# Order edges for an expert selection and full-row masks for attention and SSD scores in a two-block transformer kernel

## The chip, the cores and the metric

One core of a Trainium2 chip runs the whole program. It has TensorE (PE, matmuls), VectorE (DVE), ScalarE (ACT), GpSimd (POOL) and SyncE (SP, which issues the transfers here). The metric is the time of one execution on the device in microseconds; beside it the profiler has a span, from the first to the last instruction of one profiled execution. TensorE's granted clock is given as a share of 2.4 GHz; 0.5 is 1.2 GHz.

## The reference

One sequence of T = 256 tokens of width D = 1024 in float32 goes through two blocks, with modulation by a vector `c` in both.

```
def reference(x, ...):
    # block 1
    h  = modulate(rms_norm(x), sh1, sc1);  z = h @ w_in + b_in
    ym = mlstm(conv(mq, mk), mv, mi, mf) * sigmoid(mo)          # 4 heads of 128
    ya = moba_attention(rope(aq), rope(ak), av)                 # 8 heads of 64, one block of 256: causal softmax
    x += g1 * ((sigmoid(ga) * (ym @ p_mlstm) + sigmoid(gb) * (ya @ p_moba)) @ w_out)
    x += g2 * ((silu(h2 @ w_gate) * (h2 @ w_up)) @ w_down);  x = rms_norm(x)
    # block 2
    y_pool = pool_mixer(...)                                    # trailing-window means, 4 groups of 128
    y_ssd  = ssd_mixer(...)                                     # 16 heads of 64, two chunks of 128
        seg = a_cs[l] - a_cs[s];  decay = exp(where(l >= s, seg, -inf))
        y = (c @ b.T * decay) @ x + c @ states * exp(a_cs);  y = rmsnorm(y * silu(z))
    x += gate_m * (concat(y_pool, y_ssd) @ w_out_2)
    # PEER: 8 heads, two key tables of 128, 16384 experts
    q = h @ w_query
    v1, i1 = top_k(q1 @ keys1, 16);  v2, i2 = top_k(q2 @ keys2, 16)
    top_s, pos = top_k(v1[:, None] + v2[None, :], 16);  gates = softmax(top_s)
    x += gate_f * sum(gates * gelu(h . expert_down[idx]) * expert_up[idx]);  return rmsnorm(x)
```

## The kernel before

Nearly all of the time is matrix products with weights that are read once. SP's queue brings each weight tile, 128 x 1024 float32, to `raw` (or `ada`). Each is split: ScalarE copies it to `hi` in fp32r (L213), a rounded form of float32, and VectorE writes `lo`, the rest of `raw` less `hi` (L218). Where `cur["gp"]` is n, every n-th `lo` is made by GpSimd instead (L216). Then `proj` runs eight times three matmuls of 256 columns, `hi` by the activation's high part (L274), `hi` by its low part (L275) and `lo` by the high part (L276): 24 for a tile. The split of a tile is written two tiles ahead of its use (`LA` = 2), and the pools of `hi` and `lo` have three buffers each, so that `hi` of a tile can begin when TensorE is done with the third tile before it. `cur["lo"]` is the last `lo` of VectorE that has been written so far in the program.

In the program, smaller work is put between the weight tiles by generators: `tick()` advances the first generator in `gens` by one step, and it is called once for each tile. The order of the instructions on each engine is made by a scheduler out of a simulated timeline, and a helper `after(a, b)` adds an edge to it: `a` comes later than `b`; between instructions of one engine that is an order and no wait.

The change touches three such parts.

MoBA, `moba` (L659 on): for the second half of the tokens (`tt` = 1, 256 keys) and then the first (`tt` = 0, 128 keys), and for four pairs of heads `c`, a score of each head goes to one half `j` of a PSUM buffer `ps`. A head has 64 dimensions, and `ro` holds two heads above each other, so a score reads 64 of the 128 rows: the upper half for even `c`, the lower for odd (L671). A causal mask is added by a bfloat16 matmul of the identity with a triangle (L672). Maximum, exponential, transposes (L699 to L701), `PT` (L702) and the product with `va` (L709, L710) follow. `sg` are the gates, a sigmoid over 4096 columns on ScalarE (L107 is the helper of all exponentials and the like), and `ymH` the mLSTM's output for the product with `p_mlstm` (L731).

SSD (L860 on): for each of 16 heads a matmul over 48 rows of `ArS` selects and spreads the cumulated decays in 384 columns (L929), two bfloat16 matmuls add masks (L930, L931), and ScalarE makes the exponentials `M`. At the end of the stage come four pool products (L989), the outputs `mixS` (L1016), the sum of squares `accp` (L1021) that TensorE adds up over partitions (L1023, L1024), from it `lnt` and `srt`, with them `pv` (L1030) and `mixP` (L1031), which the last tiles of the stage multiply by weights.

PEER's selection: `topk(hq, tt)` is a generator for four heads and 128 tokens: eight rounds of max, index, replace, max, index over 128 scores (L1097 to L1101), `cand` with 256 sums for each head (L1108), four such rounds over `cand` (L1115 to L1119), index arithmetic, and the gates. There are four passes. They run beside the tiles of the query and of `dblock` (`expert_down`), 72 ticks in all; GpSimd takes part in the splits for a while. The gather stage, with `A` and `B` as one-hot masks, follows.

Of the kernel before, what the change touches and what calls it, by code (L numbers as in the profile page):

```python
# [9 lines left out]
F32 = mybir.dt.float32  # L10
# [51 lines left out]
def two_block_kernel(ctx, tc, I, out, dbg=None):  # L62
# [230 lines left out]
    gens = []  # L293

# [91 lines left out]
    with p1:  # L386
# [267 lines left out]
        identb = q1.tile([P, P], BF, name="identb")  # L654
        V.tensor_copy(identb, ident)
        trib = q1.tile([P, P], BF, name="trib")
        V.tensor_copy(trib, cs_("tri"))

        def moba():  # L659
# [4 lines left out]
            for tt in (1, 0):  # L664
                ns = (tt + 1) * P
                for c in range(4):
                    ps = sp()
                    rows = slice(64 * (c % 2), 64 * (c % 2) + 64)
                    for j in range(2):
                        r = 2 * (c // 2) + j  # L670
                        PE.matmul(ps[:, j * T:j * T + ns], ro[rows, r, tt * P:(tt + 1) * P], ro[rows, 4 + r, :ns], start=True, stop=False)  # L671
                        PE.matmul(ps[:, j * T + tt * P:j * T + ns], identb, trib, start=False, stop=True)  # L672
# [160 lines left out]
    with ExitStack() as p3:  # L833
# [48 lines left out]
        ArS = q3.tile([48, 384], F32R, name="ArS")  # L882
        id16 = q3.tile([48, 16], F32R, name="id16")
        S.activation(id16[0:32], ident[0:32, 0:16], AF.Copy)
        S.activation(id16[32:48], ident[0:16, 0:16], AF.Copy)
        identb = q3.tile([P, P], BF, name="identb")
        V.tensor_copy(identb, ident)
        trib = q3.tile([P, P], BF, name="trib")
        V.tensor_copy(trib, cs_("mB"))
# [32 lines left out]
        for i in (8, 9, 10, 11):  # L922
# [3 lines left out]
            for h in range(4 * i - 32, 4 * i - 28):  # L926
                ab = sp()
                se = id16[:, h:h + 1].to_broadcast([48, P])
                PE.matmul(ab[:, :384], se, ArS, start=True, stop=False, skip_group_check=True)  # L929
                PE.matmul(ab[:, :P], identb, trib, start=False, stop=False, skip_group_check=True)  # L930
                PE.matmul(ab[:, T:384], identb, trib, start=False, stop=True, skip_group_check=True)  # L931
# [142 lines left out]
    with ExitStack() as p4:  # L1074
# [8 lines left out]
        def topk(hq, tt):  # L1083
# [3 lines left out]
            for hf in range(2):  # L1087
# [8 lines left out]
                for h in range(4):  # L1096
                    V.max(v[:, h, 0:8], s_[:, h])  # L1097
                    V.max_index(x[:, h, 0:8], v[:, h, 0:8], s_[:, h])
                    V.match_replace(s_[:, h], v[:, h, 0:8], s_[:, h], -3.0e38)
                    V.max(v[:, h, 8:16], s_[:, h])  # L1100
                    V.max_index(x[:, h, 8:16], v[:, h, 8:16], s_[:, h])  # L1101
                    yield
# [5 lines left out]
            V.tensor_tensor(cand, vv[0].unsqueeze(3).to_broadcast([P, 4, 16, 16]),  # L1108
# [52 lines left out]
        for i in range(16):  # L1161
# [11 lines left out]
            if i == 7:  # L1173
                cur["gp"] = 2
                gens += [topk(0, 0), topk(0, 1)]
            elif i > 7:
                tick()
# [297 lines left out]
```

## Time and profile before

| | |
|---|---|
| median of 3 runs | 1427.33 us (1427.19 to 1429.57) |
| profiled execution, its own time | 1433.29 us |
| its span | 1431.5 us |
| mean granted clock | 0.989 |
| TensorE busy | 1389.7 us, 97%, 11842 matmuls |
| VectorE busy | 1155.1 us, 81% |
| ScalarE busy | 708.8 us, 50% |
| GpSimd busy | 61.3 us, 4% |
| transfers | 285.92 MB, 200 GB/s over the span |

TensorE's busy share is high over the whole, so that a change counts where it stands still or runs at half the clock: the slices of the page say where that is, the windows how much, and the waits for whom. The times of the tables are of one profiled execution, which took longer than the runs that are timed without a profile.

### The profile page before, as it was taken

How to read it: one execution, taken by the hardware profiler on the slowest of the kernel's cores; microseconds unless marked ns; L12 is line 12 of the kernel's file. 1: busy time of each engine (PE TensorE's matmuls, PEld its weight loads, DVE VectorE, ACT ScalarE, POOL GpSimd, SP SyncE). 2: the span in 40 equal slices, each digit the busy share in tenths (PEclk: the TensorE clock that was granted, in tenths of full speed). 3: DMA queues.
4: the chain of work that ended last, by engine and by line, in shares of the span. 5: the costliest groups of instructions: out<-in, count | busy, mean ns of one | idle time of the engine just before them, and what ended most of it. 6: DMA issues, size and time to landing. Idle time of an engine off the chain costs nothing.

```text
span 1431.5 us, 28913 instructions
## 1 busy us (share of the span) xinstructions
PE 1389.7 (97%) x11842; PEld 1341.2 (94%) x11842; DVE 1155.1 (81%) x1995; ACT 708.8 (50%) x1052; POOL 61.3 (4%) x50
## 2 busy tenths in 40 slices
PE   8999989999999999998899999999999999999997
PEld 6888779899999788998899999999999999999997
DVE  7999558988888597789956978989689999675554
ACT  4555465554546846555554544444444443444443
POOL 0000000000000000123420000000000000000001
PEclk9999889999999999999999999999999999999999
DMA  9988416699995353554455555555655555676663
GB/s 319 341 289 314 148 47 192 229 350 343 330 317 207 104 155 125 163 161 149 162 188 181 177 166 174 163 165 172 180 164 161 177 161 172 200 215 213 208 205 103
DMA packets 78921, 285.92 MB, mean 200 GB/s; under 512 B 8786, under 2 KB 9186, under 8 KB 78660
## 3 DMA queue, kind: packets, MB, share of 16 engines
q1 hardware_dynamic: 78484, 282.60, 60.6%
q8 instruction: 93, 1.52, 0.4%
q0 software_dynamic: 304, 1.47, 0.3%
q14 instruction: 40, 0.33, 0.1%
HBM read 282.99 MB, written 1.05 MB: 198 GB/s over the span
## 4 chain that ended last, share of the span: by engine, by line
PE 85%; DVE 10%; ACT 2%; DMA 2%; issue 1%; SPq 0%; DVEq 0%; ACTq 0%
PE pp L274 17%; PE pp L276 17%; PE pp L275 17%; PE sp L1271 9%; PE sp L1274 8%; PE sp L1275 8%; DVE lo L218 3%; PE pp L1210 2%; ACT hi L213 1%; PE sp L671 1%; DMA raw<-in_wst 0%; DVE raw L230 0%; DMA ada<-in_wst 0%; DVE M L965 0%; PE sp L929 0%
## 5 line engine op out<-in xcount | busy, mean ns | idle before, releaser
L213 ACT ACTIVATE hi<-raw 128x1024 fp32r<-128x1024 f32 x382 | 404.6, 1060 | 562.7 <-PE pp L275 282.9
L218 DVE TENSOR_TENSOR lo<-raw,hi 128x1024 fp32r<-128x1024 f32 x364 | 450.3, 1238 | 141.3 <-ACT hi L213 140.5
L276 PE MATMUL pp<-nH,lo 128*128 128x256 f32 x1064 | 301.6, 285 | 16.1 <-DVE lo L218 16.1
L274 PE MATMUL pp<-nH,hi 128*128 128x256 f32 x1064 | 300.0, 283 | 1.5 <-ACT fs L107 0.9
L275 PE MATMUL pp<-nL,hi 128*128 128x256 f32 x1064 | 300.3, 283 | 0.0
L1271 PE MATMUL sp<-wHL,hi 128*128 128x256 f32 x992 | 279.5, 283 | 0.0
L1274 PE MATMUL sp<-wHL,hi 128*128 128x256 f32 x992 | 277.7, 281 | 0.0
L1275 PE MATMUL sp<-wHL,lo 128*128 128x256 f32 x992 | 273.8, 281 | 0.0
L274 PE MATMUL pp<-hH,hi 128*128 128x256 f32 (+1 forms) x824 | 237.0, 288 | 1.3 <-ACT sg L721 1.3
L276 PE MATMUL pp<-hH,lo 128*128 128x256 f32 (+1 forms) x824 | 234.6, 285 | 0.0
L275 PE MATMUL pp<-hL,hi 128*128 128x256 f32 (+1 forms) x824 | 233.6, 284 | 0.0
L276 PEld LDWEIGHTS pp<-nH,lo 128*128 128x128 f32 x1064 | 200.2, 189 | 19.4 <-DVE lo L218 19.3
L274 PEld LDWEIGHTS pp<-nH,hi 128*128 128x128 f32 x1064 | 200.7, 189 | 2.1 <-ACT fs L107 1.1
L275 PEld LDWEIGHTS pp<-nL,hi 128*128 128x128 f32 x1064 | 200.5, 189 | 0.1
L1271 PEld LDWEIGHTS sp<-wHL,hi 128*128 128x128 f32 x992 | 188.2, 190 | 0.0
L1274 PEld LDWEIGHTS sp<-wHL,hi 128*128 128x128 f32 x992 | 188.0, 189 | 0.0
L1275 PEld LDWEIGHTS sp<-wHL,lo 128*128 128x128 f32 x992 | 185.9, 190 | 0.0
L274 PEld LDWEIGHTS pp<-hH,hi 128*128 128x128 f32 x824 | 157.1, 191 | 2.7 <-ACT sg L721 1.5
L276 PEld LDWEIGHTS pp<-hH,lo 128*128 128x128 f32 x824 | 157.2, 191 | 1.1 <-issue 0.7
L275 PEld LDWEIGHTS pp<-hL,hi 128*128 128x128 f32 x824 | 157.3, 191 | 0.7 <-issue 0.5
L1214 DVE SCALAR_TENSOR_TENSOR W<-pp,W 128x512 f32<-128x512 f32 x64 | 86.1, 1346 | 22.3 <-PE pp L1210 22.3
L213 ACT ACTIVATE hi<-ada 128x1024 fp32r<-128x1024 f32 x52 | 55.1, 1059 | 67.3 <-PE pp L275 37.9
(442 smaller groups left out, 2146.9 us busy)
## 6 DMA issues: line engine op xcount, KB each, us to landing
raw<-in_edn SPq DMA_DIRECT2D x128, 512.0 KB, 3.6
raw<-in_eup SPq DMA_DIRECT2D x128, 512.0 KB, 4.2
raw<-in_ada SPq DMA_DIRECT2D x64, 512.0 KB, 5.0
raw<-in_win SPq DMA_DIRECT2D x34, 512.0 KB, 4.4
ada<-in_ada SPq DMA_DIRECT2D x32, 512.0 KB, 5.1
raw<-in_wgu SPq DMA_DIRECT2D x32, 512.0 KB, 4.5
ada<-in_win SPq DMA_DIRECT2D x18, 512.0 KB, 4.5
raw<-in_wdn SPq DMA_DIRECT2D x15, 512.0 KB, 5.8
```

Of the source, the lines that this page charges most:

```text
L213: S.activation(hi, raw, AF.Copy)
L218: cur["lo"] = V.tensor_tensor(lo, raw, hi.bitcast(F32), OP.subtract)
L274: m = PE.matmul(ps, lh, rh, start=start, stop=False)
L275: PE.matmul(ps, lh, rl, start=False, stop=False)
L276: PE.matmul(ps, ll, rh, start=False, stop=stop)
L671: PE.matmul(ps[:, j * T:j * T + ns], ro[rows, r, tt * P:(tt + 1) * P], ro[rows, 4 + r, :ns], start=True, stop=False)
L1210: PE.matmul(ps[:, t * 64:(t + 1) * 64], A[:, t].rearrange("p n d -> p (n d)"), B[:, j, t].rearrange("p n d -> p (n d)"), start=(j == 0), s ...
L1214: V.scalar_tensor_tensor(wv, ps.rearrange("p (t n) -> p t n", t=GT), 1.0 / GSC, wv, OP.mult, OP.mult)
L1271: m = PE.matmul(o, hi[:, b], wH, start=first, stop=False, skip_group_check=True)
L1274: PE.matmul(o, hi[:, b], wL, start=False, stop=False, skip_group_check=True)
L1275: return PE.matmul(o, lo[:, b], wH, start=False, stop=last, skip_group_check=True)
```

## The change

```diff
+    def paced(ins):
+        after(ins, cur["lo"])
+        return ins
...
-        identb = q1.tile([P, P], BF, name="identb")
-        V.tensor_copy(identb, ident)
-        trib = q1.tile([P, P], BF, name="trib")
-        V.tensor_copy(trib, cs_("tri"))
+        identr = q1.tile([P, P], F32R, name="identr")
+        S.activation(identr, ident, AF.Copy)
+        trir = q1.tile([P, P], F32R, name="trir")
+        S.activation(trir, cs_("tri"), AF.Copy)
...
                 for c in range(4):
-                    ps = sp()
-                    rows = slice(64 * (c % 2), 64 * (c % 2) + 64)
-                    for j in range(2):
-                        r = 2 * (c // 2) + j
-                        PE.matmul(ps[:, j * T:j * T + ns], ro[rows, r, tt * P:(tt + 1) * P], ro[rows, 4 + r, :ns], start=True, stop=False)
-                        PE.matmul(ps[:, j * T + tt * P:j * T + ns], identb, trib, start=False, stop=True)
+                    if c % 2 == 0:
+                        pair = [sp(), sp()]
+                        for j in range(2):
+                            r = 2 * (c // 2) + j
+                            for i, ps in enumerate(pair):
+                                rows = slice(64 * i, 64 * i + 64)
+                                PE.matmul(ps[:, j * T:j * T + ns], ro[rows, r, tt * P:(tt + 1) * P], ro[rows, 4 + r, :ns],
+                                          start=j == 0, stop=False, skip_group_check=True)
+                        for ps in pair:
+                            PE.matmul(ps.rearrange("p (g s) -> p g s", g=2)[:, :, tt * P:ns], identr,
+                                      trir[:, None, :].to_broadcast([P, 2, P]), start=False, stop=True, skip_group_check=True)
+                    ps = pair[c % 2]
...
-        ArS = q3.tile([48, 384], F32R, name="ArS")
-        id16 = q3.tile([48, 16], F32R, name="id16")
+        ArS = q3.tile([P, 384], F32R, name="ArS")
+        id16 = q3.tile([P, 16], F32R, name="id16")
+        G.memset(ArS.bitcast(F32), 0.0)
+        G.memset(id16.bitcast(F32), 0.0)
...
-                se = id16[:, h:h + 1].to_broadcast([48, P])
+                se = id16[:, h:h + 1].to_broadcast([P, P])
                 PE.matmul(ab[:, :384], se, ArS, start=True, stop=False, skip_group_check=True)
-                PE.matmul(ab[:, :P], identb, trib, start=False, stop=False, skip_group_check=True)
-                PE.matmul(ab[:, T:384], identb, trib, start=False, stop=True, skip_group_check=True)
+                PE.matmul(ab.rearrange("p (g s) -> p g s", g=2)[:, :, :P], identr, trir[:, None, :].to_broadcast([P, 2, P]),
+                          start=False, stop=True, skip_group_check=True)
...
-                    V.max(v[:, h, 0:8], s_[:, h])
+                    paced(V.max(v[:, h, 0:8], s_[:, h]))
...
-                cur["gp"] = 2
+                cur["gp"] = 4
                 gens += [topk(0, 0), topk(0, 1)]
...
-            cur["gp"] = 2 if n2 < 28 else 0
+            cur["gp"] = 4 if n2 < 56 else 0
             dblock(n2)
             tick()
```

`paced` goes around all five instructions of a round over the scores, the first of each round over `cand`, `cand` itself, the first of the index arithmetic and of the gates, the first copy to `i1d`, and `A` of the gather stage. In SSD `identr` and `trir` are made as in MoBA, with the SSD's mask. The first eight tiles of the 72 are query tiles; `n2` counts the other 64. All lines behind the first edit move by 4 to 12, so that the row-half score is L677 after, the mask L680, the SSD unit L941 and L942, and the sum of squares L1035.

TensorE, at MoBA's scores, before: `ro` are the rotated queries and keys, `sp_` a PSUM buffer.

```order
L617 MATMUL sp_1293<-sq5_1291,ones_90 128x512
L671 MATMUL sp_1367<-ro_840 128x256
L672 LDWEIGHTS identb_1323
L672 MATMUL sp_1367<-trib_1325,identb_1323 128x128
L671 MATMUL sp_1367<-ro_840 128x256
```

The same place after, with the first of the following pieces of 128 columns:

```order
L621 MATMUL sp_1293<-sq5_1291,ones_90 128x512
L677 MATMUL sp_1367<-ro_840 128x256
L677 MATMUL sp_1368<-ro_840 128x256
L677 MATMUL sp_1367<-ro_840 128x256
L677 MATMUL sp_1368<-ro_840 128x256
L680 MATMUL sp_1367<-trir_1325,identr_1323 128x2x128
L680 MATMUL sp_1368<-trir_1325,identr_1323 128x2x128
...
L274 MATMUL pp_1939<-hH_85,hi_1875 128x256
L275 MATMUL pp_1939<-hL_86,hi_1875 128x256
L677 MATMUL sp_1467<-ro_840 128x128 x2
L680 MATMUL sp_1467<-trir_1325,identr_1323 128x2x128
```

Before, each score has its mask behind it. After, four scores go to two buffers in turn and two masks follow; the pieces of 128 columns come two to a buffer with projection matmuls (L274 to L276) between the buffers.

ScalarE, behind the scores, before:

```order
L702 ACTIVATE PT_1617<-sp_1623 128x384
L731 ACTIVATE ymH_2051<-hm_837 128x256 x2
L107 ACTIVATE sg_1327<-sg_1327 128x4096
L94 ACT_TABLE_LOAD
L107 ACTIVATE nfe_2068<-nfe_2068 128x8
```

and after:

```order
L712 ACTIVATE PT_1609<-sp_1615 128x384
L107 ACTIVATE sg_1327<-sg_1327 128x4096
L94 ACT_TABLE_LOAD
L107 ACTIVATE nfe_2060<-nfe_2060 128x8
L741 ACTIVATE ymH_2043<-hm_837 128x256 x2
```

The first two `ymH` have moved behind the sigmoid over `sg`.

VectorE, in the selection, from one split to the next, before (`v0`, `v1` are the values found, `x` their indices, `s` the scores):

```order
L218 TENSOR_TENSOR lo_7464<-raw_7461,hi_7463 128x1024
L1098 MAX_INDEX x0_7910<-v0_7909,s0_7902 128x8 x3
L1117 MATCH_REPLACE cand_7568<-ts__7602,cand_7568 128x256
L1098 MAX_INDEX x1_8069<-v1_8068,s1_8061 128x8 x3
L1117 MATCH_REPLACE cand_7568<-ts__7602,cand_7568 128x256
L1098 MAX_INDEX x1_8069<-v1_8068,s1_8061 128x8
L1117 MATCH_REPLACE cand_7568<-ts__7602,cand_7568 128x256 x2
L1099 MATCH_REPLACE s0_7902<-v0_7909,s0_7902 128x128 x4
L1118 MAX ts__7602<-cand_7568 128x8
L1099 MATCH_REPLACE s1_8061<-v1_8068,s1_8061 128x128 x2
L218 TENSOR_TENSOR lo_7538<-raw_7535,hi_7537 128x1024
```

and after, at the first `cand`:

```order
L218 TENSOR_TENSOR lo_7516<-raw_7513,hi_7515 128x1024
L1120 TENSOR_TENSOR cand_7546<-v0_7235,v1_7394 128x1024
L218 TENSOR_TENSOR lo_7552<-raw_7549,hi_7551 128x1024
L1127 MAX ts__7580<-cand_7546 128x8
L1128 MAX_INDEX po_7581<-ts__7580,cand_7546 128x8
L1129 MATCH_REPLACE cand_7546<-ts__7580,cand_7546 128x256
L1130 MAX ts__7580<-cand_7546 128x8
L218 TENSOR_TENSOR lo_7591<-raw_7588,hi_7590 128x1024
```

Before, two passes mix and 18 instructions stand between two splits; after, one step of one pass stands between them.

## Rows read from the trace of the kernel before

**Rows 1.** Page, 40 slices of 35.8 us, tenths
```profile
PE   8999989999999999998899999999999999999997
PEclk9999889999999999999999999999999999999999
```

**Rows 2.** Windows: length; busy PE, PEld, DVE, ACT, POOL; clock; DMA share; GB/s
```profile
161.70:167.00 5.30, 5.30 (x21) 2.63 (x20) 2.63 (x6) 3.33 (x10) 0.00 (x0) 1.00 0.27 100
167.00:184.00 17.00, 17.00 (x65) 13.15 (x65) 6.86 (x24) 8.71 (x30) 0.00 (x0) 0.50 0.10 32
556.00:563.50 7.50, 6.44 (x32) 6.34 (x32) 2.13 (x6) 1.41 (x3) 0.00 (x0) 0.54 0.26 72
617.60:728.00 110.40, 98.47 (x816) 96.85 (x815) 109.98 (x356) 56.03 (x81) 43.67 (x17) 1.00 0.46 149
1252.60:1288.40 35.80, 35.80 (x304) 35.80 (x303) 27.05 (x27) 16.24 (x16) 0.00 (x0) 1.00 0.71 215
```

**Rows 3.** Waits of TensorE, 600 to 830 us: total us, times, longest
```profile
PE pp L276 <- DVE lo L218: 11.9, 8, 2.4
```

**Rows 4.** L218 on VectorE, 617.6 to 728 us: ns minimum/median/maximum, first and last start
```profile
L218 DVE TENSOR_TENSOR lo<-raw,hi x17: 1199/1211/3262, 620.7 to 726.6; 128x1024 fp32r<-128x1024 f32 x17
```

**Rows 5.** Timeline of TensorE, end of the SSD stage: start, us, engine, line
```profile
551.88 0.59 PE L1023 MATMUL sp<-accp,ones 128*128 128x256 f32 x2
...
555.48 0.62 PE L274 MATMUL pp<-mixP,hi 128*128 128x256 f32 x3 [1.89 <-ACT mixP L1031]
```

**Rows 6.** Timeline of VectorE in the expert selection
```profile
631.00 2.88 DVE L1108 TENSOR_TENSOR cand<-v,v 128x1024 f32<-128x1024 f32 x1
...
645.05 2.23 DVE L218 TENSOR_TENSOR lo<-raw,hi 128x1024 fp32r<-128x1024 f32 x1
```

**Rows 7.** Timeline of GpSimd, same stretch
```profile
629.68 3.12 POOL L216 TENSOR_TENSOR lo<-raw,hi 128x1024 fp32r<-128x1024 f32 x1 [4.47 <-ACT hi L213]
...
643.81 2.39 POOL L216 TENSOR_TENSOR lo<-raw,hi 128x1024 fp32r<-128x1024 f32 x1 [6.04 <-ACT hi L213]
```

**Rows 8.** Timeline of TensorE, MoBA scores
```profile
161.76 0.70 PE L671 MATMUL sp<-ro 64*128 64x256 f32 x2
162.39 0.23 PE L672 MATMUL sp<-trib,identb 128*128 128x128 bf16 x1
162.55 0.70 PE L671 MATMUL sp<-ro 64*128 64x256 f32 x2
...
172.45 0.79 PE L671 MATMUL sp<-ro 64*128 64x128 f32 x2
...
173.39 0.79 PE L671 MATMUL sp<-ro 64*128 64x128 f32 x2
```

**Rows 9.** Timeline of TensorE, SSD outputs
```profile
506.32 0.65 PE L947 MATMUL sp<-M,xtok 128*64 128x256 f32 x4
506.80 0.39 PE L950 MATMUL sp<-M,xtok 128*64 128x128 f32 x4
```

**Rows 10.** Timeline of ScalarE, behind the scores
```profile
186.13 1.06 ACT L213 ACTIVATE hi<-ada 128x1024 fp32r<-128x1024 f32 x1 [0.89 <-PE pp L275]
...
188.81 3.63 ACT L107 ACTIVATE sg<-sg 128x4096 f32<-128x4096 f32 x1
```

**Rows 11.** Timeline of TensorE, behind the scores
```profile
187.99 0.65 PE L709 MATMUL sp<-PT,va 128*64 128x256 f32 x2 [1.11 <-ACT PT L702]
...
194.31 0.62 PE L274 MATMUL pp<-ymH,hi 128*128 128x256 f32 x3 [1.53 <-ACT ymH L731]
```

**Rows 12.** Timeline of TensorE, SSD masks
```profile
473.47 0.44 PE L929 MATMUL sp<-ArS,id 48*128 48x384 f32 x1
...
474.06 0.44 PE L929 MATMUL sp<-ArS,id 48*128 48x384 f32 x1
```

**Rows 13.** Waits of ScalarE, 464 to 564 us
```profile
ACT M L107 <- PE sp L931: 2.5, 3, 1.3
```

**Rows 14.** Timeline of VectorE, end of the SSD stage
```profile
549.72 0.42 DVE L1021 TENSOR_TENSOR accp<-accp,sq 128x256 f32<-128x256 f32 x1
```

More of the change, by code (lines that the diff above doesn't have):

```diff
@@ L881, in two_block_kernel @@
         cbT = q3.tile([P, 2, 384], F32, name="cbT")
-        ArS = q3.tile([48, 384], F32R, name="ArS")
-        id16 = q3.tile([48, 16], F32R, name="id16")
+        ArS = q3.tile([P, 384], F32R, name="ArS")
+        id16 = q3.tile([P, 16], F32R, name="id16")
+        G.memset(ArS.bitcast(F32), 0.0)
+        G.memset(id16.bitcast(F32), 0.0)
         S.activation(id16[0:32], ident[0:32, 0:16], AF.Copy)
         S.activation(id16[32:48], ident[0:16, 0:16], AF.Copy)
[L886 to L889, printed above, removed]
+        identr = q3.tile([P, P], F32R, name="identr")
+        S.activation(identr, ident, AF.Copy)
+        trir = q3.tile([P, P], F32R, name="trir")
+        S.activation(trir, cs_("mB"), AF.Copy)
         yv = q3.tile([P, 8, T], F32, name="yv")
@@ L1096, in topk @@
                 for h in range(4):
-                    V.max(v[:, h, 0:8], s_[:, h])
[L1098 to L1101, printed above, removed]
+                    paced(V.max(v[:, h, 0:8], s_[:, h]))
+                    paced(V.max_index(x[:, h, 0:8], v[:, h, 0:8], s_[:, h]))
+                    paced(V.match_replace(s_[:, h], v[:, h, 0:8], s_[:, h], -3.0e38))
+                    paced(V.max(v[:, h, 8:16], s_[:, h]))
+                    paced(V.max_index(x[:, h, 8:16], v[:, h, 8:16], s_[:, h]))
                     yield
@@ L1107, in topk @@
             cand = w4.tile([P, 4, 16, 16], F32, name="cand")
-            V.tensor_tensor(cand, vv[0].unsqueeze(3).to_broadcast([P, 4, 16, 16]),
-                            vv[1][:, :, None, :].to_broadcast([P, 4, 16, 16]), OP.add)
+            paced(V.tensor_tensor(cand, vv[0].unsqueeze(3).to_broadcast([P, 4, 16, 16]),
+                            vv[1][:, :, None, :].to_broadcast([P, 4, 16, 16]), OP.add))
             yield
@@ L1114, in topk @@
                 ch = cand[:, h].rearrange("p a b -> p (a b)")
-                V.max(ts_[:, h, 0:8], ch)
+                paced(V.max(ts_[:, h, 0:8], ch))
                 V.max_index(po[:, h, 0:8], ts_[:, h, 0:8], ch)
@@ L1124, in topk @@
                 if hf == 0:
-                    V.tensor_scalar(ju, pof, 4, None, op0=OP.logical_shift_right)
+                    paced(V.tensor_scalar(ju, pof, 4, None, op0=OP.logical_shift_right))
                 else:
-                    V.tensor_scalar(ju, pof, 15, None, op0=OP.bitwise_and)
+                    paced(V.tensor_scalar(ju, pof, 15, None, op0=OP.bitwise_and))
                 jf = w4.tile([P, 64, 2], F16, name="jf")
@@ L1137, in topk @@
             ga_ = gat[tt][:, hs]
-            V.tensor_tensor(ga_, ts_, ts_[:, :, 0:1].to_broadcast([P, 4, 16]), OP.subtract)
+            paced(V.tensor_tensor(ga_, ts_, ts_[:, :, 0:1].to_broadcast([P, 4, 16]), OP.subtract))
             act(ga_, ga_, AF.Exp)
@@ L1148, in topk @@
                     PE.transpose(tp[:, j * P:(j + 1) * P], a, ident)
-                V.tensor_copy(i1d[:, tb], tp[:, 0:P].unsqueeze(2).to_broadcast([P, P, 2]))
+                paced(V.tensor_copy(i1d[:, tb], tp[:, 0:P].unsqueeze(2).to_broadcast([P, P, 2])))
                 V.tensor_copy(i2d[:, tb], tp[:, P:T].unsqueeze(2).to_broadcast([P, P, 2]))
@@ L1197, in gstage @@
             A = q5.tile([P, GT, 64, 2], F16, name="A")
-            V.tensor_tensor(A, iob.rearrange("p (n d) -> p n d", d=2)[:, None].to_broadcast([P, GT, 64, 2]),
-                            i1d[:, tsl, None, :].to_broadcast([P, GT, 64, 2]), OP.is_equal)
+            paced(V.tensor_tensor(A, iob.rearrange("p (n d) -> p n d", d=2)[:, None].to_broadcast([P, GT, 64, 2]),
+                                  i1d[:, tsl, None, :].to_broadcast([P, GT, 64, 2]), OP.is_equal))
             yield
```

## The prediction

> **What bounds the kernel now.** The page first: by its slices TensorE is at 9 tenths nearly everywhere and the granted clock at 9, TensorE with an 8 in the sixth slice (179 to 215 us) and in the nineteenth and twentieth (644 to 716), the clock with an 8 in the fifth and sixth (143 to 215) [rows 1]. A stretch of 35.8 us from the last third, read with the view by windows, shows a full TensorE: busy 35.80 of 35.80 with 304 matmuls, so 0.118 us for one projection matmul and 24 x 0.118 = 2.83 us for a weight tile [rows 2]. Nothing on another engine can shorten such a stretch; only matmuls left out, TensorE's own gaps and its clock count. The gaps lie in three places, and the change has a part for each.
>
> The largest is the expert selection. Between 617.60 and 728.00 TensorE works 98.47 of 110.40 us, VectorE 109.98 [rows 2]. The chain of waits names one thing: L276, the matmul that reads `lo`, waits for VectorE's L218 eight times, 11.9 us in all [rows 3]. A split itself takes 1.21 us at the median, but up to 3.26 [rows 4]. So VectorE is full, with top-k instructions queued ahead of splits that TensorE needs.
>
> The second is MoBA's scores. From 161.70 the clock is full, from 167.00 to 184.00 it is 0.50 throughout, that is 1.2 GHz, with 65 matmuls in 17 us [rows 2]. What TensorE did before it fell was a run of score units, a 64-row matmul and a 128-row mask each.
>
> The third is the end of the SSD stage: a gap of 1.89 us before the first matmul on `mixP`, and then 0.54 of the clock from 556.00 to 563.50 [rows 2, 5].
>
> **Term 1, the paced selection: about -11.5 us.** An order edge costs no time of its own: the instruction only stands behind the last emitted split on the same queue. What it removes is what stands ahead: in the rows of VectorE in the change section a split stood behind 18 top-k instructions, and up to 26 elsewhere in this stage; now 0 to 12 stand between two splits. What limits this is the work itself. Before, three of four passes were done in this stretch: 110.4 less 17 splits of 1.21 leaves 89.8, or 29.9 for one pass, what GpSimd's presence costs included. Four passes are 120 us, now spread over the 72 tiles of the stage: 1.66 for a tile. GpSimd now takes every fourth split instead of every second, so VectorE has 3/4 x 1.21 = 0.91 more: 2.57 of TensorE's 2.83 us. VectorE fits, with 0.26 a tile to spare. The densest four tiles of the new order come to an estimated 10.8 to 11.0 of 11.3.
>
> The loss inside this is the contention of the two engines that split. While GpSimd's split ran from 629.68 for 3.12 us, a `cand` of VectorE took 2.88, and while one ran from 643.81 for 2.39, a split of VectorE took 2.23 instead of 1.21 [rows 6, 7]. So one GpSimd split costs VectorE 1.0 to 1.7 us. There are about 16, as before (18), but now over the whole stage. A split has slack: `hi` and `lo` have three buffers, `hi` of tile i may start when tile i-3 is done, which leaves two tiles, 5.66, less 1.06 for `hi` and 1.21 for `lo`: 3.4 us. A hold of 1.7 fits in it and is caught up within the next tiles if each has 0.26 and more. I take a rest of 0.4 of the 11.9; bounds 0 and 11.9 (all of it stays).
>
> Does the longer presence of GpSimd speak against this? In the rows the held `cand` and the held split both end 1.08 us after GpSimd's split does (632.80 and 646.20), so they stood still until then [rows 6, 7]. A split of GpSimd begins when its `hi` is there and is over 2.39 later; the next split of VectorE needs the next `hi`, 2.83 later in a full stretch. So it should find the way free, and only a `cand` or a like operation is caught. The Trainium skill has a rule here (SBUF — State Buffer, section on its ports): VectorE, with two inputs from SBUF, and GpSimd take a shared pair of ports as a lock, held for the whole instruction, while the other blocks. The trace agrees by the two ends named. By the rule at its worst, with VectorE caught at each start, all 16 splits would hold it 2.39 us, and the sum would come out as in the fourth rival.
>
> **Term 2, the score pairs: about -7 us.** Before, a unit (score and mask) starts every 0.79 us at full clock (161.76 to 162.55) and every 0.94 at half, with 128 instead of 256 columns (172.45 to 173.39) [rows 8]. TensorE's order before is 16 such units with 52 projection matmuls between them, from 161.76 to 186.05: 24.3 us, of it 17 at half clock. After, the same part holds 61 (nine that stood ahead, worth 1.1 at full clock), so the like of it before is 25.4.
>
> Now four scores alternate between row halves, and two masks follow, each for both pieces of its buffer. (A float32 matmul leaves two records in the trace.) The trace before has no alternating halves of rows. The nearest rows are those of L947, two float32 matmuls of 256 columns that alternate in column halves: 0.48 us until the next starts [rows 9]. For four scores of 256 columns the bounds are therefore 0.96 (as L947) and 2.52 (four one after the other, each 0.63 from 161.76 to the mask at 162.39 [rows 8]). I take 1.25, nearer the lower end, because L947 too keeps both halves of the array at work. The masks are float32r of 256 columns, 0.12 each by [rows 2], and 0.11 for the changeover: 1.6 us for the six instructions (1.3 to 2.9), against 4 x 0.79 = 3.16 before. The pieces of 128 columns come two scores and a mask at a time, not alternating, because the second buffer isn't free yet; two half-clock units of 0.94 take 0.94 at full clock, so 1.05 with a changeover. That makes 2 x 1.6 + 4 x 1.05 + 61 x 0.118 = 14.6 us, if the clock stays: 10.8 less than 25.4.
>
> Not all of it arrives. Behind it ScalarE has a sigmoid over 4096 columns of 3.63 us [rows 10], and TensorE waited 1.11 for `PT` and 1.53 for `ymH` there [rows 11]. In the order of after, no `ymH` stands ahead of that sigmoid any more (two did), so TensorE, earlier by ten, runs out of work and waits for about the sigmoid: 3.8 to 5 us in place of the 1.53. At 3.8, 2.3 of the 10.8 are given back and 8.5 remain. If the clock falls in this wait, about 3 more go. I take 7, bounds 3 and 8.5.
>
> **Term 3, the SSD masks and the end of the stage: about -4 us.** A unit of three matmuls takes 0.59 us (473.47 to 474.06) [rows 12]; after it is 384 and 256 columns in full rows, 0.178 + 0.118 = 0.30 by the pitch of [rows 2]. Sixteen save 4.6 us of TensorE. But ScalarE, which waited for these only 2.5 us in all [rows 13], takes over as the bound; and four copies to `identr` and `trir` are on ScalarE instead of VectorE: by width an eighth of the 1.06 of `hi` [rows 10], with a fixed part an estimated 0.25 each. So 1.5 to 2.5 arrive; I take 1.7. The zeroing of `ArS` and `id16` is on GpSimd, idle here: nothing; without that cover 384/1024 of a split's 2.39, 0.9 us.
>
> At the end, the sum of squares is written at 549.72 + 0.42, but L1023 runs at 551.88, behind 44 projection matmuls since the last pool matmul, and what is left then is too short to cover the chain to `mixP` [rows 5, 14]. In the order of after only 18 stand between. So 26 x 0.118 = 3.1 us move behind it and cover the 1.89: 2.3 with the smaller stops after it. If the clock then holds, up to 3.3 more. Bounds of the whole term 2 and 6.
>
> **What costs nothing.** SP's order is the same, row for row, so no transfer moves. In the gather stage `A` stands behind a split; TensorE is full there [rows 2] and VectorE is busy 27.05 of 35.80. The feed-forward part keeps its order.
>
> **The sum.** 11.5 + 7 + 4 = 22.5. The profiled execution took 1433.29 us (span 1431.5), so it would take 1410.8. The median of the runs is 6 us lower, without a profile: 1427.33 - 22.5 = 1404.8, **1405 us**.
>
> **The rivals.**
> First, **the clock doesn't hold** (18%): score pairs or the longer wait behind the sigmoid still drop it, as the run of units does now; terms 2 and 3 give 3 and 2 or less. 11.5 + 5 = 16.5: 1411.
> Second, **the selection still stalls** (10%): VectorE is at 98% of the stage already, and the pacing puts its work behind splits which themselves wait for `hi`; half the 11.9 stays, spread over the 72 tiles, and with terms 2 and 3 below their middle, 7 of 11, that is 6 + 7 = 13, 1414. For it speaks that 0.26 a tile is little; against it, that the fourth pass now shares the later tiles.
> Third, **nothing measurable** (4%): the stalls move and only the score unit's 3 to 5 us come, given back by longer waits at `mixP` and `ymH`: 1426.
> Fourth, **slower** (4%): the place is each of the 16 GpSimd splits in tiles 167 to 227. If it holds VectorE for its whole 2.39 and the spare of a period of four tiles (4 x 0.26 = 1.0) takes up only that, each leaves 1.4 us of lateness, which TensorE waits out once the slack of 3.4 is used up; with the held top-k work behind it up to 1.8 each. The old 11.9 go, terms 2 and 3 still give 11, so from (11.9 + 11) / 16 = 1.43 us a split it decides against the change; at 1.8 the time is 1427.3 - 22.9 + 28.8 = 1433. Against it: the holds read were 1.0 and 1.7, not 2.39 [rows 6], and most top-k instructions weren't held.
> The likeliest (64%) is all three terms: 1398 to 1410.
>
> **Range and chances.** Low end: 11.9 + 8.5 + 6 plus 4 for a clock that holds: 1397. High end: takes in the first two rivals: 1417. Beyond are the last two and a little on the low side, under 2 in 10. A measurement of this kernel can't tell less than 0.2%, 2.9 us, from no change. Faster 0.92, within 0.04, slower 0.04.
>
> **What would show it.** Right: between the start of the query tiles and tile 232 hardly a wait of L276 for L218; score pairs without the half clock; the SSD unit at a pitch of 0.30; the sum-of-squares matmuls ahead of the last 26. Wrong: waits of TensorE for `lo` beside GpSimd splits, or a clock of 0.5 after 165 us as before; a pair unit of over 2.5 us; a wait for `ymH` of over 5.

## The result, and the profile after

The change takes 1410.35 us at the median of 4 runs (1408.62 to 1413.79), before 1428.45 beside it: a ratio of 0.987, 95% interval 0.984 to 0.990, 18 us less. It was forecast at 1405, with a range of 1397 to 1417. The profiled execution took 1408.62 us, span 1406.8, against 1433.29 and 1431.5 before: 24.7 us, more than the runs show: the execution of before that was profiled took longer than any of the four runs beside the change (1427.19 to 1433.03), and that of the change is the fastest of its four.

The slices of the page, as in [rows 1]:

```profile
PE   8999989999999998999999999999999999999997
PEclk9999999999999999999999999999999999999999
```

The two 8s of TensorE at the selection are 9s now, and the clock's 8s are gone. The 8 of the sixth slice (176 to 211 us) has stayed: the waits behind the scores lie there. A new 8 stands in the sixteenth (528 to 563), at the end of the SSD stage.

The view by windows, columns as in [rows 2]: the scores, the projections behind them, the two stretches of lower clock that follow, the end of the SSD stage, and 110.4 us of the selection from the same distance behind its first matmul as the row of before.

```profile
159.50:167.00 7.50, 7.50 (x54) 6.06 (x53) 4.11 (x13) 5.23 (x20) 0.00 (x0) 1.00 0.22 71
167.00:172.00 5.00, 5.00 (x38) 4.49 (x37) 2.91 (x8) 4.49 (x16) 0.00 (x0) 1.00 0.02 3
176.00:181.00 5.00, 3.89 (x14) 2.44 (x14) 3.77 (x10) 5.00 (x6) 0.00 (x0) 0.66 0.16 53
183.00:187.00 4.00, 4.00 (x18) 3.01 (x18) 1.54 (x5) 1.70 (x6) 0.00 (x0) 0.57 0.00 0
545.00:550.00 5.00, 4.56 (x24) 4.35 (x23) 1.35 (x2) 1.06 (x1) 0.00 (x0) 0.62 0.05 20
603.90:714.30 110.40, 110.40 (x933) 110.40 (x932) 95.12 (x288) 60.03 (x89) 22.25 (x10) 1.00 0.57 179
```

Through the scores the clock is 1.00, where it was 0.50 for 17 us. It still falls behind them, to 0.66 and 0.57, and at the end of SSD, to 0.62. In the selection TensorE is busy 110.40 of 110.40, and VectorE, which had 109.98, only 95.12.

Waits of TensorE over the whole program, as in [rows 3]: total, times, longest.

```profile
PE pp L276 <- DVE lo L218: 4.3, 5, 2.2
...
PE sp L719 <- ACT PT L712: 2.2, 1, 2.2
PE pp L274 <- ACT mixP L1043: 1.9, 1, 1.9
PE pp L274 <- ACT ymH L741: 1.8, 1, 1.8
PE pp L1222 <- DVE A L1210: 1.8, 3, 0.6
```

L276 waits 4.3 us for VectorE's split in the whole program, none of it in the selection. The stop at `mixP` has its old length [rows 5], the one at `ymH` went from 1.53 to 1.8 and that at `PT` from 1.11 to 2.2 [rows 11]. New is the last line: the gather stage waits for `A`.

### The profile page after: what moved, and what is told of

Its sections match the earlier page's. It is cut to its first block, busy times and chain, and to the rows that moved or that the text cites. A ratio compares the mean times of both kernels' runs of the same rounds, so it can differ in the third digit from the quotient of the medians.

```text
span 1406.8 us, 28875 instructions
## 1 busy us (share of the span) xinstructions
PE 1372.1 (98%) x11818; PEld 1333.5 (95%) x11818; DVE 1156.1 (82%) x1993; ACT 709.5 (50%) x1056; POOL 53.8 (4%) x50
## 3 DMA queue, kind: packets, MB, share of 16 engines
HBM read 282.99 MB, written 1.05 MB: 202 GB/s over the span
## 4 chain that ended last, share of the span: by engine, by line
PE 59%; DVE 1%; issue 0%; ACT 0%; DVEq 0%; ACTq 0%
PE pp L274 10%; PE pp L275 10%; PE pp L276 10%; PE sp L1283 9%; PE sp L1287 9%; PE sp L1286 9%; PE pp L1222 2%; PE sp L1104 1%; DVE lo L218 0%; PE sp L1327 0%; DVE A L1210 0%; ACT hi L213 0%; DVEq L1473 0%; DVE xT L1335 0%; DVE B L1214 0%
## 5 line engine op out<-in xcount | busy, mean ns | idle before, releaser
L218 DVE TENSOR_TENSOR lo<-raw,hi 128x1024 fp32r<-128x1024 f32 x366 | 446.7, 1221 | 133.2 <-ACT hi L213 131.8
L276 PE MATMUL pp<-nH,lo 128*128 128x256 f32 x1064 | 302.2, 285 | 4.5 <-DVE lo L218 4.3
L274 PE MATMUL pp<-nH,hi 128*128 128x256 f32 x1064 | 301.2, 284 | 2.4 <-ACT fs L107 0.9
L1287 PE MATMUL sp<-wHL,lo 128*128 128x256 f32 x992 | 276.7, 281 | 0.0
L274 PE MATMUL pp<-hH,hi 128*128 128x256 f32 (+1 forms) x824 | 236.1, 287 | 0.0
L276 PE MATMUL pp<-hH,lo 128*128 128x256 f32 (+1 forms) x824 | 232.4, 283 | 0.0
L276 PEld LDWEIGHTS pp<-nH,lo 128*128 128x128 f32 x1064 | 201.6, 190 | 6.3 <-DVE lo L218 6.1
L274 PEld LDWEIGHTS pp<-nH,hi 128*128 128x128 f32 x1064 | 201.2, 190 | 3.3 <-ACT fs L107 1.1
L274 PEld LDWEIGHTS pp<-hH,hi 128*128 128x128 f32 x824 | 155.4, 189 | 1.3 <-issue 0.8
L276 PEld LDWEIGHTS pp<-hH,lo 128*128 128x128 f32 x824 | 155.4, 189 | 0.6 <-issue 0.2
```

What stands on the lines that cost most here:

```text
L218: cur["lo"] = V.tensor_tensor(lo, raw, hi.bitcast(F32), OP.subtract)
L274: m = PE.matmul(ps, lh, rh, start=start, stop=False)
L276: PE.matmul(ps, ll, rh, start=False, stop=stop)
L1287: return PE.matmul(o, lo[:, b], wH, start=False, stop=last, skip_group_check=True)
```

## The experiments

Every kernel was profiled and timed beside the kernel before on the same chip. For each, the table has the lengths of four stages, from first and last starts of their matmuls in the profile: the scores (first score to the last product with `va` over 256 columns), SSD (first mask unit to first key product), the selection (first key product to first one-hot product), the gather stage (first to last one-hot product). A single profile's scores and SSD stages vary with the clock falls that it has; the other two had full clock, but for one fall in e6 (at 705.8 us, in the selection), and repeat within a microsecond where the code is the same.

| kernel | median us | ratio to before (95%) | scores | SSD | selection | gather |
|---|---|---|---|---|---|---|
| before | 1428 to 1431 | | 43.9 | 121.6 | 245.4 | 372.1 |
| the change | 1410.35 | 0.987 (0.984 to 0.990) | 36.0 | 120.5 | 232.1 | 374.5 |
| e8, the change again | 1410.76 | 0.984 (0.981 to 0.987) | 36.0 | 119.8 | 232.1 | 374.5 |
| e1, selection part | 1418.59 | 0.992 (0.990 to 0.994) | 42.5 | 121.4 | 232.1 | 374.5 |
| e2, scores part | 1421.74 | 0.995 (0.993 to 0.996) | 35.9 | 120.5 | 244.8 | 372.1 |
| e3, SSD part | 1424.77 | 0.996 (0.995 to 0.997) | 42.4 | 116.9 | 245.8 | 372.1 |
| e4, change, A free | 1408.49 | 0.984 (0.982 to 0.985) | 37.0 | 119.8 | 231.8 | 372.1 |
| e5, pacing alone | 1415.80 | 0.988 (0.985 to 0.991) | 42.8 | 121.4 | 230.9 | 372.1 |
| e6, GpSimd's rule alone | 1430.13 | 0.998 (0.996 to 1.000) | 43.9 | 122.0 | 244.0 | 372.1 |
| e7, scores not alternating | 1422.09 | 0.992 (0.989 to 0.995) | 36.0 | 122.0 | 245.7 | 372.1 |
| e9, grouped, old masks | 1423.92 | 0.996 (0.994 to 0.997) | 36.4 | 121.3 | 245.8 | 372.1 |
| e10, change, edges only | 1407.98 | 0.984 (0.983 to 0.986) | 35.9 | 118.7 | 230.9 | 372.1 |
| e11, e10 and ymH first | 1402.02 | 0.980 (0.979 to 0.982) | 33.4 | 119.5 | 230.9 | 372.1 |
| e12, pacing, no GpSimd | 1419.05 | 0.992 (0.989 to 0.994) | 45.3 | 121.5 | 231.2 | 372.1 |

### The three parts apart: e1, e2, e3

Each is the kernel before with one part of the change's diff: `paced`, all its uses and the two lines of `cur["gp"]` (e1); the `moba` part (e2); the `ArS`, `id16`, `identr` and `trir` of SSD (e3).

Expected of e1: 

> Only the paced selection, the gather stage's edge and GpSimd's every fourth split; scores and SSD masks as before. If the profile of the change is read rightly, the stage from the first key product to the first one-hot product is shorter by 13.3 us, no wait of L276 for L218 is left in it, and the gather stage gives back 2 to 2.5 us: 10.5 to 11.5 us less than before. Rival: part of the 13.3 comes from the stages ahead (TensorE reaching the selection with splits further along); then the stage alone gives under 8 us.

Measured: 0.992, so 11.7 us (9 to 15). The selection is 13.3 us shorter and the gather stage 2.4 longer. The theory holds and the rival falls: the whole 13.3 lie in the selection's own stage.

Expected of e2: 

> Only the MoBA scores in alternate row halves with full-row masks. From the profile of the change: TensorE reaches the end of the stage about 10 us earlier, of it 2.5 us because the clock is full again when the feed-forward part starts, so 8 to 11 us less than before. Rival: the 1.6 us that were gained ahead of the scores in that profile came with this part and not from run to run, and the clock's two falls in the waits behind the sigmoid give back more when the rest of the program is as before: 4 to 6 us less.

Measured: 9.6 us at the medians, 7.9 by the fast runs' ratio (5 to 10), and 8.0 in the stage. It lies at the theory's lower end; the 2.5 us that the first profile showed behind this stage didn't come again as a part of it.

Expected of e3: 

> Only the SSD masks in full rows, float32r. Theory from the profile of the change: the mask units save 3.4 us at the last unit, and the wait of L276 for a split behind xtok, 2.2 us with a clock of 0.65 after it, and the unchanged stop at mixP take most of it back: 0 to 2 us less. Rival, the forecast's term: 4 us less, 2 to 6.

Measured: 0.996, so 5.6 us (4 to 8), and 4.7 in its profile's stage. For this kernel the forecast's term is right and the theory taken from the first profile is not. But over the profiles the stage is 119.2 in the mean of the six kernels with the part (116.9 to 120.5) and 121.5 in the eight without it (120.5 to 122.0): 2.3 us. The trace of e3 shows why it has more than the change: 15 projection matmuls stand between the sum of squares and `mixP`, where the change and before have 6, and TensorE waits 1.33 and 0.67 us for `mixP` instead of 1.87 and 1.07; it has no wait ahead of the first key product, where the change has 0.71; and its falls of the clock cost 1.7 us less. Together these are 3.4 of the 3.6 by which its stage is shorter than the change's.

The three add up: 11.7 + 7.9 + 5.6 = 25 by the ratios, against 23 for the change in e8 (19 to 28) and 18 in its first timing (14 to 23). For e8 a sum of 22 to 25 had been expected, and 18 by the rival that the parts share what they gain: e8 speaks for the sum, the first timing for the rival, and their intervals overlap.

### The edge of A: e4

```diff
-            paced(V.tensor_tensor(A, iob..., OP.is_equal))
+            V.tensor_tensor(A, iob..., OP.is_equal)
```

Expected: 

> The change without the order edge of A in the gather stage; all else as changed. Theory: that edge alone delays A, the 1.8 us of waits for A go, and the time is 2 to 2.5 us below that of the change, 20 us below before. Rival: the gather stage loses its 2.5 us because it starts with other distances between splits, whatever the edge: within 0.5 us of the change, 18 us below before.

Measured: 1408.49, ratio 0.984, so 23 us (21 to 26). The gather stage has its 372.1 us again, as in every kernel without the edge, and 374.5 in the three with it. So the edge costs 2.4 us in the profiles, and the rival falls. The timings don't tell it: the ratio is 0.984 here (0.982 to 0.985) and 0.984 in e8 (0.981 to 0.987). With the edge, the change has three stops, 51.3 us apart, of which this is the first (in brackets what the product waited for, and how long):

```profile
864.81 0.55 PE L1222 MATMUL pp<-B,A 128*128 128x64 f16 x13 [0.60 <-DVE A L1210]
```

### Pacing or GpSimd's rule: e5, e6, e12

e5 has the edges of the selection with the old rule of GpSimd; e6 has only the two lines of the rule; e12 is e5 with

```diff
-                cur["gp"] = 2
+                cur["gp"] = 0
...
-            cur["gp"] = 2 if n2 < 28 else 0
+            cur["gp"] = 0
```

Expected of e5: 

> Only the order edges (with that of A); GpSimd takes every second split over the first 28 dblock tiles as before. In the order between two splits of VectorE at most 11 top-k instructions stand, 26 before. Theory, the bunches cause the waits: the selection stage gives 10 us or more of the 13.4 and the waits of L276 for L218 fall under 2 us, the time is 8 to 11 below before. Rival, VectorE's load: behind the 28 tiles it has 1.66 + 1.21 = 2.87 us of work for a tile of 2.83 and no help, so waits return in the later tiles: 6 us or more of them, the stage gives 4 to 7.

The kernel that ran did not have the edge of A, other than this says. Measured: the selection takes 230.9, 14.4 us less than before, without any wait for a split; 0.988 in the timing, 17 us (13 to 21).

Expected of e6: 

> Only GpSimd's every fourth split over 56 dblock tiles, without an order edge. Up to 19 top-k instructions stand between two splits. Theory, the bunches cause the waits: half of them stay, 4 to 8 us of waits of L276 for L218, the stage gives 4 to 8. Rival, the spread of GpSimd's help alone settles it: under 2 us of waits, the stage gives 11 or more.

Measured: the selection gains 1.3 us, with a fall of the clock in it that costs 1.7; in the timing it is 3 us (0.4 to 6), hardly clear of noise. The waits of TensorE in this stage:

```profile
PE pp L276 <- DVE lo L218: 4.7, 5, 1.2
PE pp L276 <- POOL lo L216: 3.3, 2, 2.5
```

8.0 us stay, of which GpSimd's own split now has 3.3 (one took 4.67 us instead of 2.39). The theory's upper end for the waits holds, and the gain, at most 3.0 without the fall, is below its lower end. The rival falls: spread over more tiles, the help removes a third of the waits.

Expected of e12: 

> Only the selection's order edges, without that of A, and no split on GpSimd at all. Theory: a GpSimd split holds VectorE for about as long as it saves (1.0 to 1.7 against 1.21), so the 89.8 us of three passes hold some 20 us of standing still, a pass alone takes 23, and four with all splits are 1.3 + 1.21 = 2.5 of 2.83 a tile: no waits, the stage as with order edges alone, 231 us. Rival, the load of the forecast: 1.66 + 1.21 = 2.87 of 2.83, waits return, 3 to 8 us more in the stage.

Measured: 231.2, as with GpSimd's help. One stretch of 110.4 us of the selection in e5 and the same in e12, by windows:

```profile
612.80:723.20 110.40, 110.40 (x933) 110.40 (x933) 95.17 (x286) 60.19 (x89) 44.13 (x18) 1.00 0.56 179
```

```profile
618.60:729.00 110.40, 110.40 (x934) 110.40 (x933) 101.66 (x298) 60.31 (x89) 0.00 (x0) 1.00 0.59 182
```

TensorE is full in both. e5 has 18 splits on GpSimd there. On VectorE 18 splits would be 21.8 us at 1.21, but VectorE is busy only 6.5 us more (101.66 less 95.17), and 7.0 over the whole stage, where it has just 18 instructions more. So each GpSimd split had cost VectorE some 0.8 us of standing in its instructions (14.8 / 18), and gave it 1.21. The instructions that stand are mostly casts now, and no longer splits; here one kind of cast over this stage in e5 and then in e12 (busy us, mean ns of one, idle us before them):

```profile
L1108 DVE CAST xf<-x 128x64 f16<-128x64 uint32 x8 | 8.3, 1035 | 0.1
```

```profile
L1108 DVE CAST xf<-x 128x64 f16<-128x64 uint32 x8 | 1.5, 189 | 0.1
```

And the load without help, 101.66 of 110.40, is 2.61 us for a tile, not the 2.87 that the rival took from the forecast. By time e12 gains 12 us (8 to 16) and e5 17 (13 to 21), which aren't told apart.

### What makes the scores quick: e7, e9

e7 is e2 with the two loops exchanged, so that both scores of one row half come first and then both of the other:

```diff
-                        for j in range(2):
-                            r = 2 * (c // 2) + j
-                            for i, ps in enumerate(pair):
-                                rows = slice(64 * i, 64 * i + 64)
+                        for i, ps in enumerate(pair):
+                            rows = slice(64 * i, 64 * i + 64)
+                            for j in range(2):
+                                r = 2 * (c // 2) + j
```

Expected: 

> Only the scores' part, with the masks in full rows, but the two scores of one row half one behind the other instead of the halves in turn. Theory, the overlap of the two halves is worth what the pitch says: four scores of 256 columns take 2.2 to 2.5 us instead of 1.06, so 2.3 to 3 us more than with alternation in two such units, and the clock stays full through the scores. Rival, the clock hangs on the overlap: it falls to 0.5 within the scores as before and 5 us or more of the 8 go again.

e9 is e2 with the masks of before behind the four scores:

```diff
-                        for ps in pair:
-                            PE.matmul(ps.rearrange(...)[:, :, tt * P:ns], identr, trir..., start=False, stop=True, ...)
+                        for ps in pair:
+                            for j in range(2):
+                                PE.matmul(ps[:, j * T + tt * P:j * T + ns], identb, trib, start=False, stop=j == 1, ...)
```

Expected: 

> Only the scores' order: four scores, halves in turn, and behind them four bfloat16 masks as before, one for each score, in place of one float32r mask for two. Theory, what counts is that a 64-row score no longer stands between 128-row masks: four scores take 1.06 us as in the change, the clock stays full through the scores, 7 to 8 us less than before. Rival, the masks' kind counts: the clock falls in the scores again and under 3 us are left.

TensorE's timeline at the first four scores (eight records) in the change:

```profile
159.54 1.13 PE L677 MATMUL sp<-ro 64*128 64x256 f32 x8
160.60 0.50 PE L680 MATMUL sp<-trir,identr 128*128 128x256 f32 x2
161.04 1.13 PE L677 MATMUL sp<-ro 64*128 64x256 f32 x8
...
162.90 0.71 PE L677 MATMUL sp<-ro 64*128 64x128 f32 x4
163.54 0.38 PE L680 MATMUL sp<-trir,identr 128*128 128x256 f32 x1
163.76 0.28 PE L276 MATMUL pp<-hH,lo 128*128 128x256 f32 x1
...
173.72 0.30 PE L709 MATMUL sp<-cst,P 128*128 128x128 f32 x1
```

in e7:

```profile
160.03 1.14 PE L673 MATMUL sp<-ro 64*128 64x256 f32 x8
161.10 0.50 PE L676 MATMUL sp<-trir,identr 128*128 128x256 f32 x2
161.53 1.14 PE L673 MATMUL sp<-ro 64*128 64x256 f32 x8
```

and in e9:

```profile
161.57 1.14 PE L673 MATMUL sp<-ro 64*128 64x256 f32 x8
162.63 0.40 PE L677 MATMUL sp<-trib,identb 128*128 128x128 bf16 x4
162.96 1.13 PE L673 MATMUL sp<-ro 64*128 64x256 f32 x8
```

Four scores take 1.06 us in the change, 1.07 in e7 without alternation, 1.06 in e9. Two float32r masks take 0.44 (160.60 to 161.04), the four bfloat16 masks 0.33. Before, one score took 0.63 to its mask [rows 8], so four took 2.52. So neither the order of the halves nor the kind of mask is the cause; what the three have in common is that the scores come four together, two of each half, and that a 128-row mask no longer follows each 64-row score.

That e7 is as quick doesn't mean that the halves don't overlap. The timeline of one instant, 0.02 us behind the start of the first score, shows how many of its records have begun (the last number): one before, two in the change, two in e7, and one in the change's pieces of 128 columns, where both scores are of the same half. In this order:

```profile
161.76 0.48 PE L671 MATMUL sp<-ro 64*128 64x256 f32 x1
```

```profile
159.54 0.49 PE L677 MATMUL sp<-ro 64*128 64x256 f32 x2
```

```profile
160.03 0.49 PE L673 MATMUL sp<-ro 64*128 64x256 f32 x2
```

```profile
162.90 0.37 PE L677 MATMUL sp<-ro 64*128 64x128 f32 x1
```

So both halves run at the same time in e7 too, although its order has both scores of one half first. By these rows the gain has two parts. With both halves at once, 1.06 is the time of two scores of one half: 0.63 for the first, as before, and 0.43 for the second, with no mask between them. Four grouped scores without overlap would be an estimated 0.63 + 3 x 0.43 = 1.92. Of the 1.46 saved, some 0.6 would then come from the grouping and 0.86 from the overlap. No run takes the overlap away, so this division is argued and not shown.

Of e7's expectation neither side came: the four scores aren't slower, and the clock doesn't fall. Of e9's the theory holds, with 6 us instead of 7 to 8 (in its interval). For the clock, windows over the scores, with the old scores in e1 (the second line is the fall), and over the same part in e7 and in e9:

```profile
161.00:165.00 4.00, 4.00 (x16) 2.01 (x16) 2.23 (x5) 2.26 (x6) 0.00 (x0) 1.00 0.46 131
167.00:180.00 13.00, 13.00 (x49) 9.89 (x49) 4.03 (x11) 5.67 (x25) 0.00 (x0) 0.50 0.13 42
```

```profile
160.00:175.00 15.00, 14.98 (x107) 12.71 (x107) 9.47 (x27) 12.19 (x40) 0.00 (x0) 1.00 0.24 74
```

```profile
161.00:176.00 15.00, 14.22 (x108) 11.31 (x106) 9.50 (x28) 12.17 (x40) 0.00 (x0) 1.00 0.30 81
```

In all six profiles with the old scores the clock falls between 164 and 167 us and stays at half for 13.6 us or more; in none of the eight with grouped scores does it fall within them, and the first fall behind them is at 176 or later. Whether it is the change between 64 and 128 rows or the longer run of such units that lowers it isn't told apart. By time, e7 gains 11 us (7 to 16), e2 8 (5 to 10), e9 6 (4 to 8); the three aren't told apart beyond that.

### Without A's edge and the new rule, and with one edge more: e10, e11

e10 is the change without A's edge and with GpSimd's old rule. e11 adds an edge on ScalarE:

```diff
-            S.activation(ymH[:, h], hm[:, h], AF.Copy)
+            yc = S.activation(ymH[:, h], hm[:, h], AF.Copy)
...
-        act(sg, sg, AF.Sigmoid)
+        after(act(sg, sg, AF.Sigmoid), yc)
```

Expected of e10: 

> The change without the edge of A and with GpSimd's splits as before (every second, 28 tiles). Theory from the selection's and the gather's stages in the kernels so far: 2.4 us from A's edge and 1 us from GpSimd's rule less than the change, 24 to 26 below before. Rival, a clock fall of 1.7 us more or less hides it: 20 to 23 below before.

Measured: 1407.98, ratio 0.984, 22 us less (20 to 25): the rival's range and the theory's lower end; it isn't told from e4.

Expected of e11: 

> As the kernel above, and an edge that keeps the sigmoid over sg behind the last ymH. Theory, the wait for ymH (1.8 to 3.2 us) goes, and the clock falls behind it (1.7 us each) become fewer: 2 to 5 us less than the kernel above. Rival, ScalarE is full there: the sigmoid then stands ahead of the later PT copies and the gates' product, TensorE waits for these instead: within 1 us.

Measured: 1402.02, ratio 0.980 (0.979 to 0.982), 6 us below e10 beside it. Waits of TensorE between 140 and 240 us in e10 and then in e11:

```profile
PE sp L719 <- ACT PT L712: 2.2, 1, 2.2
PE pp L274 <- ACT ymH L741: 1.9, 1, 1.9
```

```profile
PE sp L719 <- ACT PT L712: 2.2, 1, 2.2
PE pp L274 <- ACT hi L213: 1.4, 3, 0.6
```

The wait for `ymH` is gone and `PT`'s is as long as it was; TensorE has 29 projection matmuls on `ymH` to do (184.43 to 187.98) while ScalarE ends the sigmoid and makes the next `PT`. The theory holds and the rival falls. The stage is 2.5 us shorter. Of the rest the two profiles show 0.9 ahead of the scores and 2.9 between MoBA and SSD, where e10 waits 1.67 us for a split (276.9) and then has a fall of the clock, and e11 waits 0.49; 0.8 go back in SSD. Whether the edge is the cause of that isn't shown. The change itself was not run beside e11.

## Why the prediction was right, step by step

**The selection (-11.5 forecast).** Mechanism and size hold: the waits of L276 fell from 11.9 us to none, the stage from 245.4 to 232.1. But the sum was right by two errors that cancel, and that is luck. "`A` stands behind a split; TensorE is full there" was taken as free; the edge costs 2.4 us (e4), of which 1.8 are the three stops of a one-hot product for its `A`. The step that failed is the row that it was read from: 1252.60 to 1288.40 lies behind the gather stage (840.5 to 1212.6). In that stage VectorE had less room than 27.05 of 35.80:

```profile
900.00:1000.00 100.00, 100.00 (x1050) 99.26 (x1049) 89.24 (x121) 42.61 (x64) 0.00 (x0) 1.00 0.56 168
```

And the stage gave 13.3, not 11.5: a stop costs TensorE more than its row.

```profile
639.88 0.39 PE L276 MATMUL pp<-nH,lo 128*128 128x256 f32 x1 [1.18 <-DVE lo L218]
640.10 0.28 PE L274 MATMUL pp<-nH,hi 128*128 128x256 f32 x1
```

The row counts from the end of the matmul ahead, which is drawn 0.28 us long where the pitch is 0.118, and the first matmul behind the stop is followed 0.22 later (639.88 to 640.10). That is some 0.27 more for each stop, and 14.1 for the eight; with GpSimd's old rule the edges gave 14.4 (e5). Net of `A`, the change gave 10.9.

GpSimd's new rule, which the forecast used to make VectorE's work fit ("2.57 of 2.83"), does nothing: with the old rule 230.9, without GpSimd 231.2, with the new one 232.1 (e5, e12, e1). The step that failed is the work of a pass, 29.9 us, read from a stretch in which VectorE stood in held instructions: the four `cand` had a median of 1.78 us before and 1.22 after. Without GpSimd the top-k work is 1.40 us a tile (2.61 less 1.21), so about 25 for a pass; with the new rule VectorE's whole load is 2.44 a tile (95.12 of 110.40), not 2.57. The fourth rival's mechanism is real, at some 0.8 us for a split, but VectorE has room for it. The Trainium skill (SBUF — State Buffer, section on its ports) would have VectorE wait out the rest of GpSimd's instruction; [rows 6, 7] agree, and the mean loss of 0.8 is a third of a split's 2.39.

**The scores (-7 forecast).** The size holds: 7.9 in the stage of the change's profile, 6.4 to 9.4 against all profiles with the old scores. So does the mechanism. The pair unit took 1.50 us (forecast 1.6) and the pieces of 128 columns 0.86 (162.90 to 163.76; forecast 1.05). From the first score to the first transpose, at 173.72, it is 14.2 us, forecast 14.6, where before took 24.3 with nine projection matmuls fewer. Behind it TensorE waits 2.21 + 1.81 = 4.0 where it had waited 2.64, and the wait that the forecast had at 3.8 to 5, for `ymH`, is 1.81; `PT`'s, which it left as it was, has doubled. The price was taken from two column halves at work at the same time, and the row halves do overlap. What the forecast had wrong is that they must alternate in the order: they need not (e7). And it had no term of its own for the grouping (e9). The Trainium skill (TensorEngine Tiling (Array Packing), Key Properties) says that a change of tiling mode drains TensorE. The trace agrees with that: a score with a 128-row mask behind it took 0.63, a second one of the same half behind it 0.43 more. Its rule that different tiles work in parallel is seen too: two records start within 0.02 us, with halves in turn (159.54) and with one half first (160.03).

The first rival, that the clock falls again behind the sigmoid, is half true: it falls there twice, 1.7 us each (176 to 181, 183 to 187), and not in the scores. e11 shows the wait for `ymH` to be avoidable.

**SSD (-4 forecast).** The mask unit is 0.29 us, forecast 0.30:

```profile
460.89 0.34 PE L941 MATMUL sp<-ArS,id 128*128 128x384 f32 x1
461.06 0.28 PE L942 MATMUL sp<-trir,identr 128*128 128x256 f32 x1
461.18 0.34 PE L941 MATMUL sp<-ArS,id 128*128 128x384 f32 x1
```

From the first unit to the last it is 14.1 us instead of 17.5: 3.4, twice the 1.7 that was taken, so ScalarE held it up less than thought. But then TensorE waits for a split whose `hi` stands behind nine activations of ScalarE and whose `lo` stands behind `xtok` on VectorE, and the clock falls behind it:

```profile
487.32 0.58 PE L276 MATMUL pp<-nH,lo 128*128 128x256 f32 x1 [2.23 <-DVE lo L218]
```

It was 1.52 there before. So 2.3 of the 3.4 stay in the mean. The second part of the term failed altogether: the stop at `mixP` is 1.87 instead of 1.89, and the sum of squares stands as late as it did.

```profile
537.40 0.59 PE L1035 MATMUL sp<-accp,ones 128*128 128x256 f32 x2
...
541.00 0.61 PE L274 MATMUL pp<-mixP,hi 128*128 128x256 f32 x3 [1.87 <-ACT mixP L1043]
```

The count was right, 18 projection matmuls instead of 44 between the last pool matmul and L1035, and the conclusion wrong: the pool matmul has moved back, not the sum of squares forward; six matmuls are left behind it, as before. The distance should have been counted to the instruction that waits, the first matmul on `mixP`. Nor do the SSD masks make this order: e2, which has only the scores' part, has 14 there, with the same six behind the sum and the same stop (1.86).

**The sum.** Forecast 22.5; by stages 10.9 + 7.9 + 1.1 = 19.9 in the first profile; 18 (14 to 23) and, in e8, 23 (19 to 28) in the timings. The time itself came out at 1410.35, 5 us over the forecast and nearest to the first rival's 1411; but that rival's parts, 3 for the scores and 2 for SSD, are not what came. The largest miss of a term is SSD, 1.1 to 2.3 instead of 4. The rest of that profile's 24.7 lies outside: 2.2 ahead of the scores, and 2.5 between MoBA and SSD, where the profile of before had one more fall of the clock (0.53 from 212 to 215) and this one had none.

## What to carry to other kernels

When an engine is nearly always busy in a stage and late for the one that counts, look first at the order in its queue: here the same work, put between the splits instead of ahead of them, removed every wait, while the help of a third engine, spread over more tiles, removed a third of them, and taking that help away from the paced order brought none back. Matmuls that use half the rows should be written together, those of both halves in one group, with the full-row ones behind all of them; that took four scores from 2.5 to 1.06 us and kept the clock. An order edge is not free where the paced instruction feeds the bound engine itself: put it on what is early, never on what is awaited.

## What the runs showed of the hardware

Falls of the clock go with most of what differs between executions of one kernel: over the 38 executions of the kernel before that have a clock on record (1427.0 to 1436.8 us), time and loss, (1 - mean clock) x span, have a correlation of 0.79, at 0.8 us of time for 1 us of loss. Summed as (1 - clock) over windows of 1 us up to 620 us, the profile of before lost 13.6 us, that of the change 8.5, e2's 3.4 and e12's 17.0; the one in the old scores cost 6.8 to 10.2 in the six profiles that have it, the others 1.7 to 5.1 each. Some come at the same place in all profiles with one form of the code (the old scores), others (85 to 90 us in e8, e9 and e12, 456 to 471 in six kernels) in some only. So a single pair of profiles can be off by several us, and stages at full clock are the better measure. How much of the difference between the profiles' 24.7 and the runs' 18 is clock isn't shown: the runs of before beside the change have no clock on record.
